# A streaming encoder layer on one core: when the operand sums of the output projection begin, and how two input projections are cut

## The chip, the cores and the metric

The kernel runs on one core of one Trainium2 chip. The time is the device time of one execution in microseconds (us); lower is better. A core has a matrix engine (TensorE, "PE" in the profile, with its weight loads as "PEld"), a vector engine (VectorE, "DVE"), a scalar engine (ScalarE, "ACT"), GpSimd ("POOL") and a queue that issues transfers (SyncE, "SP").

## The reference

One layer of a hybrid encoder, for 2048 prompt rows and 64 rows of a running stream, with model width 1024:

```python
aq, ak, av, ag, hq, hf, hi, hg = jnp.split(rms_norm(x, ln_g) @ w_in, SPLITS, axis=-1)
k, v = heads(ak), heads(av)
o_a = attn_fn(heads(aq), k, v).reshape(B, T, W_A) * jax.nn.silu(ag)
o_b, S = hgrn2_branch(hq, hf, hi, hg, lb, norm_g, s0)
y = x + jnp.concatenate([o_a, o_b], axis=-1) @ w_out
...
y_prompt, y_sample = rms_norm(hp, ln_f_g), rms_norm(hs, ln_f_g)
```

The input projection is 1024 by 4096 (eight groups of 512 columns). `attn_fn` is banded attention, 8 heads of 64, each 64-row chunk seeing itself and eight chunks before. `hgrn2_branch` is a gated linear recurrence with 4 heads of 128, whose gate is made of `hf` and whose query of `hq`. The output projection is 1024 by 1024, followed by the residual and a final RMS norm. New keys, values and recurrent states are outputs too. All arrays are float32; the kernel gets that accuracy by splitting each operand into a high part and a low remainder and adding three products.

## The kernel before

**Super-blocks and jobs.** The 2112 rows are worked in four super-blocks: 512, 576 (512 prompt rows and the 64 stream rows), 512 and 512. Each has 32 jobs, one for each 128 columns of the input projection. Job 0 is `hf` of head 0 (the forget gate), job 1 is `hq` of head 0 (the query). `project` (line 539) makes one job: 24 matmuls of 128 by 128 by the rows of a piece, 8 with the high weights and the high part `xh` of the normalized rows, 8 with the low part `xl`, 8 with the low weights and `xh`. The result goes to one of two accumulators `acc`, and a thread then moves it out of there: `ev_f` (line 1268) for `hf`, `silu_to` (line 566) for `hq`. Most jobs of the super-blocks of 512 rows are one piece of 512.

**The seam between two super-blocks.** `xh` and `xl` have one buffer. The rows of the next super-block are transposed into it in tiles of 128 rows (`x_tile`, line 351, and `x_split`, line 404: ACT writes `xh` on line 409, DVE writes `xl` on line 415) as soon as the last two jobs of this one have read their half (`x_left`). So the last two jobs of a super-block and the first two of the next are cut into halves of 256 rows (256 and 320 in the second super-block) and interleaved: job 0 half 0, job 1 half 0, job 0 half 1, job 1 half 1 (line 2092, with `u == 1`). `x_ready` (line 425) holds each of these pieces until the rows it reads are there.

**The output projection.** It is made for eight pairs of 128-row tiles (`pairs`, number i), each as a product of 2 by 2 blocks with seven block products instead of eight (`NPROD`, number k). For each pair four blocks a11, a12, a21, a22 are loaded; products 0, 1 and 6 read the blocks a11, a12 and a22 as loaded, and four sums are made in the same buffers:

- a11 = a11 - a21 on POOL, two instructions of 128 by 256
- a21 = a21 + a22 on DVE, one instruction of 128 by 512
- s2 = a22 - a11 on POOL, two instructions
- a12 = a12 - s2 on POOL, two instructions

Product 2 reads s2, product 3 the new a21, products 4 and 5 the new a11 and a12. For each product, `out_parts` (line 1729) has ACT copy the block to its high part (line 1751), and `out_low` (line 1755) subtracts it for the low part (line 1759): on POOL in two halves for pairs 0 and 1 except product 3, on DVE for the others. The sums stand at the end of `out_low`, under `k == 1`: the thread of product 1 makes them, on lines 1772 (DVE) and 1777 (POOL), and then marks them done in `sums_at`, for which the copy for product 2 waits. `out_step` (line 1821) makes 12 matmuls of 512 columns for each product, in the order of `steps` (line 1640): the products of pairs 0 and 1 interleaved, then pair by pair. `out_adds` (line 1859) adds a product to the residual rows (line 1847) or to a shared sum (lines 1865, 1873, 1852), and `out_norm` (line 1892) does the final norm (lines 1901 to 1926) and the store.

**Who sets the order.** The engines' instruction orders are written out when the program is made. A planner (`Plan`, line 52) keeps a clock of its own; every piece of work is a generator thread that yields what it waits for: a time, a token of a buffer, a condition, or a pair such as ("D", t), which means "time t, and DVE's queue no longer than 800 ns" (`QUEUE`). `pump` goes on with every thread whose wait is over, in the order of priority and then of age. The main thread, which issues the projections and the output products, lets the others in after every two matmuls. The planner's costs (`act`, `dve`, `pool`, `mm`) set the order alone; what the chip waits for are the data. So a thread that goes on earlier in the planner's clock puts its instructions further ahead in the queues of its engines, and everything after may fall in another order.

## Time and profile before

| | us |
|---|---|
| median of 3 runs | 1245.14 |
| lowest and highest | 1242.21, 1245.45 |
| the profiled execution | 1244.75 |
| its span, first to last instruction | 1243.0 |

| engine | busy us | share of the span | instructions |
|---|---|---|---|
| PE | 1229.9 | 99% | 7398 |
| PEld | 1079.5 | 87% | 7398 |
| DVE | 896.0 | 72% | 1897 |
| ACT | 680.2 | 55% | 1526 |
| POOL | 415.7 | 33% | 702 |

In rows of the timeline and the groups, "L1759" is line 1759, the name left of the arrow is the tile written, those right of it are read, and numbers in brackets at the end are idle time of the engine before the row and what ended it. A matmul's row gives its whole passage through the array, of which the next one overlaps a part; what a matmul costs in a stream is the distance from one start to the next. The projections of the third super-block start at about 539 us, those of the fourth at about 800 us; the output products run from 1056 us on, at first between the last attention blocks, from 1097 us on alone, and the last ends at 1236 us.

### The profile page before, as it was taken

To read this page: it belongs to the slowest core of one execution; us is meant where nothing else is said; L and a number is where in the kernel's file an instruction comes from. 1 tells how busy PE (TensorE), PEld (TensorE's weight loads), DVE (VectorE), ACT (ScalarE), POOL (GpSimd) and SP (SyncE) were. 2 spreads that over 40 slices of the span, in tenths; PEclk is the share of its full clock that TensorE was granted. 3 is DMA by queue.
4 is the path that set the end of the run, shared out by engine and by line. 5 is a ranking of instruction groups with operands and counts; after the bars stand their busy time and mean duration, and the time that the engine had idled before them with its cause. 6 is when DMAs were issued, how large, how long until landed. Compare 5 with 4: busy or idle time off the path is not lost.

```text
span 1243.0 us, 21228 instructions
## 1 busy us (share of the span) xinstructions
PE 1229.9 (99%) x7398; PEld 1079.5 (87%) x7398; DVE 896.0 (72%) x1897; ACT 680.2 (55%) x1526; POOL 415.7 (33%) x702
## 2 busy tenths in 40 slices
PE   9999999999999999999999999999999999999997
PEld 7888888999999999998888888988888888778786
DVE  7687878867767677786577667785768566866775
ACT  6354546755565556674455656664646444643443
POOL 7665564111120111201243242143242203664543
PEclk9999999999999999999999999999999999999999
DMA  8897988667575476655777878778878676987441
GB/s 338 302 321 258 322 292 330 204 183 253 155 219 147 153 248 197 197 165 188 274 270 252 283 264 266 238 245 270 272 274 249 222 244 211 352 257 225 128 136 67
DMA packets 158324, 294.36 MB, mean 237 GB/s; under 512 B 51657, under 2 KB 98377, under 8 KB 140554
## 3 DMA queue, kind: packets, MB, share of 16 engines
q1 hardware_dynamic: 157784, 292.74, 70.4%
q8 instruction: 58, 0.95, 0.3%
q14 instruction: 48, 0.39, 0.1%
q10 hardware_dynamic: 434, 0.27, 0.1%
HBM read 198.52 MB, written 95.49 MB: 237 GB/s over the span
## 4 chain that ended last, share of the span: by engine, by line
PE 92%; DMA 4%; DVE 3%; ACT 1%; issue 0%; SPq 0%; DVEq 0%; ACTq 0%
PE acc L249 61%; PE g L249 9%; PE pv L249 7%; PE tr L253 6%; PE s L249 5%; PE tr L249 3%; DMA out_dram<-ck 1%; DMA way<-vT 1%; DMA vT<-way 1%; PE g L253 1%; DMA w<-wd 0%; DMA mixd<-mixa 0%; DMA lbg<-in_lb_gamma_dram 0%; DMA bias<-wind 0%; ACT ck L1901 0%
## 5 line engine op out<-in xcount | busy, mean ns | idle before, releaser
L249 PE MATMUL acc<-xh,w 128*128 128x512 f32 (+2 forms) x2720 | 564.2, 347 | 0.8 <-ACT xh L409 0.7
L249 PEld LDWEIGHTS acc<-xh,w 128*128 128x128 f32 x2720 | 435.4, 189 | 51.6 <-ACT xh L409 0.9
L249 PE MATMUL acc<-xl,w 128*128 128x512 f32 (+2 forms) x1360 | 291.4, 346 | 0.5 <-DVE xl L415 0.5
L249 PEld LDWEIGHTS acc<-xl,w 128*128 128x128 f32 x1360 | 220.5, 189 | 26.5 <-DVE xl L415 0.7
L948 DVE CUSTOM_DVE_ANT_0 pr<-s,bias 128x640 f32<-128x640 f32 (+4 forms) x128 | 94.2, 736 | 53.1 <-PE s L249 52.6
L977 ACT CAST ph<-tr 128x512 fp32r<-128x512 f32 (+3 forms) x176 | 88.0, 506 | 75.6 <-PE pv L249 45.2
L965 ACT ACTIVATE pr<-pr,nm 128x640 f32<-128x640 f32 (+4 forms) x132 | 100.3, 760 | 52.4 <-DVE nm L948 52.0
L473 POOL TENSOR_TENSOR w<-wraw,w 128x256 fp32r<-128x256 f32 x120 | 102.3, 882 | 55.1 <-DVE w L468 41.8
L980 DVE TENSOR_TENSOR ph<-tr,ph 128x512 fp32r<-128x512 f32 (+3 forms) x176 | 100.8, 588 | 21.5 <-ACT ph L977 20.9
L249 PE MATMUL pv<-ph,v 128*128 128x256 f32 (+2 forms) x344 | 97.7, 370 | 0.9 <-DVE sm L968 0.7
L253 PE MATMUL tr<-ident,pr 128*128 128x128 f32 x580 | 88.3, 273 | 0.0
L1596 POOL TENSOR_TENSOR k<-ob 128x512 f32<-128x512 f32 (+2 forms) x20 | 18.0, 902 | 201.2 <-ACT ob L1587 163.2
L1121 POOL TENSOR_TENSOR mixa<-mixa,sga 128x256 f32<-128x256 f32 (+1 forms) x36 | 28.5, 792 | 167.9 <-DVE mixa L1019 142.2
L510 POOL TENSOR_TENSOR xn<-wraw,xn 128x256 fp32r<-128x256 f32 x48 | 40.2, 838 | 132.9 <-ACT xn L507 132.9
L969 DVE TENSOR_SCALAR pr<-pr,sm 128x640 f32<-128x640 f32 (+4 forms) x132 | 76.6, 580 | 4.7
L1019 DVE TENSOR_TENSOR mixa<-mixa,pv 64x256 f32<-64x256 f32 (+1 forms) x144 | 56.8, 394 | 30.7 <-ACT mixa L1015 27.1
L253 PEld LDWEIGHTS tr<-ident,pr 128*128 128x128 f32 x580 | 69.6, 140 | 10.3 <-DVE ph L980 1.1
L575 ACT ACTIVATE sig<-acc 128x512 f32<-128x512 f32 (+2 forms) x63 | 31.8, 505 | 73.4 <-PE acc L249 72.6
L249 PEld LDWEIGHTS pv<-ph,v 128*128 128x128 f32 (+1 forms) x344 | 58.3, 189 | 9.4 <-ACT pr L965 1.1
L1015 ACT COPY mixa<-pv 64x256 f32<-64x256 f32 (+1 forms) x72 | 25.1, 349 | 60.6 <-PE pv L249 54.7
L249 PE MATMUL s<-kd,q 128*128 128x320 f32 (+2 forms) x232 | 55.8, 311 | 0.2 <-DVE nm L948 0.2
L249 PE MATMUL s<-kd,ql 128*128 128x320 f32 (+2 forms) x232 | 55.5, 309 | 0.0
(414 smaller groups left out, 2126.0 us busy)
## 6 DMA issues: line engine op xcount, KB each, us to landing
w<-wd SPq DMA_DIRECT2D x96, 1024.0 KB, 5.8
wd<-w SPq DMA_DIRECT2D x32, 1024.0 KB, 7.1
wraw<-in_w_in_dram SPq DMA_DIRECT2D x30, 512.0 KB, 4.7
wod<-xn SPq DMA_DIRECT2D x28, 512.0 KB, 5.0
xn<-in_x_prompt_dram SPq DMA_DIRECT2D x23, 512.0 KB, 5.1
bias<-biasd SPq DMA_DIRECT2D x24, 320.0 KB, 5.7
carry<-kd SPq DMA_DIRECT2D x12, 512.0 KB, 6.2
carry<-v SPq DMA_DIRECT2D x12, 512.0 KB, 6.3
```

The lines of the kernel that those rows point to most:

```text
L249: pe.matmul(out, w, x, **kw)
L253: pe.transpose(out, x, idn)
L473: pool.tensor_sub(w[:, 1, k : k + 2], raw[:, k : k + 2], f32(w[:, 0, k : k + 2]))
L510: pool.tensor_sub(f32r(st[:, c.start + 512 : c.stop + 512]), src[:, c], st[:, c])
L575: act.activation(sig[:, :bn], acc, AF.Exp, scale=-1.0)
L948: dve.tensor_tensor_reduce(s[:, :nk].rearrange("p (a c) -> p a c", a=ns), sps[:, :ns, :kn], d.bias[:, h, bcol : bcol + nk].rearrange("p (a ...
L965: act.activation(s[:, :nk], s[:, :nk], AF.Exp, bias=nm[:, 0:1], scale=-1.0, accum_out=sm)
L969: dve.tensor_scalar(s[:, :nk], s[:, :nk], sm, None, ALU.mult)
L977: act.copy(ph[:krows, 0, :wid], pt[:krows, :wid])
L980: dve.tensor_sub(ph[:krows, 1, :wid], pt[:krows, :wid], f32(ph[:krows, 0, :wid]))
L1019: dve.tensor_add(mix[hs, :qn], mix[hs, :qn], pv[hs, i, :qn])
L1121: pool.tensor_mul(mix[:, :n], mix[:, :n], d.sg[:, g0 : g0 + n])
```

## The change

In the output projection the four sums move from the thread of product 1 to that of product 0, and only the last of them (into a12, which product 1 reads) still waits for product 1's low part. In the third and fourth super-block (`sb > 1`) job 0 is made alone in its two halves, and job 1 after it in one piece of 512; the first two super-blocks and the last two jobs of each stay as they were.

```diff
@@ out_low
         if k == NPROD - 1:
             for tag, n in tags.items():
                 tk[tag].put(n, t)
-        if k == 1:
+        if k == 0:
             (a11, a12, a21, a22), s2 = rows_at[i][:2]
-            yield lambda: (i, 0) in a_at
             for out, x, y, op in ((a11, a11, a21, ALU.subtract), (a21, a21, a22, ALU.add),
                                   (s2, a22, a11, ALU.subtract), (a12, a12, s2, ALU.subtract)):
                 if op == ALU.add:
...
                     dve.tensor_tensor(out, x, y, op)
                     C.dve(560, t)
                     continue
+                if out is a12:
+                    yield lambda: (i, 1) in a_at
                 for c in (slice(0, 2), slice(2, 4)):
                     yield "P", 0.0
                     pool.tensor_tensor(out[:, c], x[:, c], y[:, c], op)
@@ program
-                if u == 1 or (u == len(JOBS[sb]) - 1 and not last):
+                if sb > 1 and u == 0:
+                    for half in range(2):
+                        yield from project(j, [halves[half]], evac, half == 1,
+                                           lambda part, k0: x_ready(sb, half, part, k0))
+                elif u == 1 and sb < 2 or u == len(JOBS[sb]) - 1 and not last:
                     for half in range(2):
                         yield from project(j - 1, [halves[half]], before, half == 1,
                                            lambda part, k0: x_ready(sb, half, part, k0))
```

## The prediction, on record before the change was run

> **What bounds the kernel now.** I read the engines' busy times first, then what the matrix engine (PE) waited for, then stretches of time, then the order of time around the two places that the change touches.

> ```profile
> span 1243.0 us, 21228 instructions
> PE 1229.9 (99%) x7398; PEld 1079.5 (87%) x7398; DVE 896.0 (72%) x1897; ACT 680.2 (55%) x1526; POOL 415.7 (33%) x702
> ...
> PE 92%; DMA 4%; DVE 3%; ACT 1%; issue 0%; SPq 0%; DVEq 0%; ACTq 0%
> ```

> PE is busy in all but 13 us, and 92% of the chain that ended last is PE. So time can be won only by fewer or cheaper matmuls, or out of PE's few waits:

> ```profile
> PE acc L249 <- DVE slot L1759: 1.8, 1, 1.8
> ...
> PE pv L249 <- DVE sm L968: 0.7, 1, 0.7
> PE acc L249 <- ACT xh L409: 0.7, 2, 0.5
> PE acc L249 <- DMA w<-wod: 0.6, 1, 0.6
> ```

> The columns are total us, times, longest. The largest belongs to an output product that waited for a low part on DVE (L1759). The next two tables are of stretches: length, then busy time of PE, PEld, DVE, ACT and POOL, the granted clock, and the transfers.

> ```profile
> 538.00:558.00 20.00, 20.00 (x160) 19.61 (x159) 16.96 (x46) 15.63 (x39) 1.05 (x5) 1.00 0.50 161
> 800.00:820.00 20.00, 20.00 (x155) 19.33 (x155) 17.60 (x41) 16.76 (x42) 2.49 (x3) 1.00 0.76 243
> ...
> 830.00:1070.00 240.00, 238.40 (x1322) 201.48 (x1322) 159.98 (x317) 127.24 (x257) 67.95 (x106) 1.00 0.78 255
> ...
> 1116.20:1119.60 3.40, 1.61 (x7) 1.14 (x7) 3.40 (x6) 1.77 (x4) 0.00 (x0) 1.00 0.75 214
> 1119.60:1123.00 3.40, 3.40 (x10) 2.62 (x9) 2.42 (x6) 1.34 (x3) 0.06 (x1) 0.51 0.89 320
> 1123.00:1126.40 3.40, 3.40 (x16) 2.78 (x16) 1.48 (x3) 0.62 (x1) 3.40 (x5) 0.99 0.84 253
> ```

> At the two seams that the change cuts anew PE has no idle time at all. At 1116 us it idles, and right after that the granted clock is 0.51 for 3.4 us: 10 matmul records against 16 in the stretch behind it. The waits of 0.7 and 0.6 us (on L968 and on the transfer `w`) lie between 830 and 1070 us, where the clock stays at 1.00. So this one wait costs 1.8 us and about 3.4 x 0.49 = 1.7 us more, 3.5 us together.

> **Part 1, job 1 in one piece.** It takes 24 pairs of 256-column matmuls away in each of two super-blocks and puts 48 matmuls of 512 columns in their place. The price of each is read from the chain of waits, where these rows are unbroken streams: the first consists of 512-column matmuls alone, the second of 256-column ones.

> ```profile
> 563.87 8.64 PE acc L249 x38
> ...
> 807.43 3.35 PE acc L249 x28
> ```

> 8.64 / 38 = 227 ns, and 3.35 / 28 = 120 ns; two halves cost 239 ns against 227. 48 x 12 ns = 0.57 us are saved, all on the path, since PE is never idle there. [...]

> What it adds is a stricter order. Job 0's second half now follows its first half at once, where job 1's first half stood between them: 24 x 0.120 = 2.9 us less for the rows of the second half to arrive. In the fourth super-block they arrive so (PE's job 0 first, then the last writes of `xh` and `xl`):

> ```profile
> 800.40 1.11 PE L249 MATMUL acc<-xh,w 128*128 128x256 f32 x8
> 801.36 1.12 PE L249 MATMUL acc<-xl,w 128*128 128x256 f32 x8
> ...
> 803.83 1.43 PE L249 MATMUL acc<-xh,w 128*128 128x256 f32 x10
> ...
> 804.11 0.59 ACT L409 CAST xh<-g 128x512 fp32r<-128x512 f32 x1
> ...
> 804.44 0.69 DVE L415 TENSOR_TENSOR xl<-tr,xh 128x512 fp32r<-128x512 f32 x1
> 805.05 0.68 DVE L415 TENSOR_TENSOR xl<-g,xh 128x512 fp32r<-128x512 f32 x1
> ```

> Job 0's first half ends with the second matmul of the row at 803.83, at 804.07. Its second half would need the last piece of `xh` four matmuls later, at 804.55 (there at 804.70), the first of `xl` at 805.18 (there at 805.13), the last of `xl` at 805.66 (there at 805.73): 0.2 us of waits if nothing else stood between. In the third super-block the same margins are as close; I bound both seams together at 0 below, because score and transpose matmuls of the last attention pair stand between today and can go on doing so, and at 0.57 above, the whole of this part's gain. I take 0, being nearest to the stretches in which PE idles 0.00 us of 20. If that cover were gone, the loss is the 0.2 us per seam just worked out.

> Around it: `hq` is moved out of `acc` as one piece and not two, so the recurrence of head 0 begins a little later; the instructions saved are on ACT and DVE, which are not the bound. The accumulator turns over one time less, and job 0's weight buffer comes free a half-job (2.9 us) earlier, so the next weights are issued on SP no later than now. I put no cost or gain on these: PE's other work, 20.00 us in 20, hides them; without that cover the late `hq` would cost one extra half-piece on ACT and DVE, below 1 us.

> **Part 2, the sums.** No instruction is added or removed: six POOL pieces and one DVE sum per pair. They are put further ahead in the queues, by at most the time between the low parts of products 0 and 1. Where can that reach PE? Only where a low part came late, and there is one such place, product 2 of pair 2, which reads s2:

> ```profile
> 1109.09 0.68 DVE L1759 TENSOR_TENSOR xl<-wraw,xh 128x512 fp32r<-128x512 f32 x1
> ...
> 1109.91 1.77 POOL L1777 TENSOR_TENSOR wraw<-wraw,wraw 128x256 f32<-128x256 f32 x2 [5.84 <-DVE xl L1759]
> 1111.64 1.88 POOL L1777 TENSOR_TENSOR sga<-wraw,wraw 128x256 f32<-128x256 f32 x2
> ...
> 1114.81 0.57 ACT L1865 COPY asb<-pv 128x512 f32<-128x512 f32 x1
> 1115.27 0.62 ACT L1751 CAST slot<-sga 128x512 fp32r<-128x512 f32 x1
> ...
> 1115.22 1.76 DVE L1926 SCALAR_TENSOR_TENSOR bias<-bias,rstd,gin 128x1024 f32<-128x1024 f32 x1
> 1116.91 0.68 DVE L1847 TENSOR_TENSOR pr<-pr,pv 128x512 f32<-128x512 f32 x1
> 1117.51 0.68 DVE L1759 TENSOR_TENSOR slot<-sga,slot 128x512 fp32r<-128x512 f32 x1
> ...
> 1115.97 0.48 PE L249 MATMUL acc<-w,slot 128*128 128x512 f32 x1
> 1118.24 3.89 PE L249 MATMUL acc<-w,slot 128*128 128x512 f32 x11 [1.79 <-DVE slot L1759]
> ```

> Here `sga` is s2. POOL already starts the first sum 0.13 us after product 0's low part ends (1109.77), so as data s2 cannot come earlier: the move gains nothing on POOL. s2 is complete at 1113.52, but ACT copies it at 1115.27 and DVE subtracts it at 1117.51. In between stand the norm of pair 1 and the sums of pair 2 (L1865 on ACT; L1926, 1.76 us, and L1847, 0.60 us to the next start, on DVE). That is a matter of order. In the planner's costs one copy and one subtraction part the two low parts, but the copies were issued together here, so the sums come about half a microsecond earlier in the planner's clock. That is of the size that lets s2's low part pass one neighbour. The bounds: 0 if it passes none, -3.5 us if it passes both DVE neighbours (it then starts near 1115.9, when the copy is done, the wait falls below the 0.7 us waits that left the clock whole, and the half clock goes with it). I take one neighbour, L1847: -0.60 us, half clock kept. For pairs 3 to 7 PE shows no wait in the list above, so an earlier s2 is worth nothing.

> For pairs 0 and 1 the low parts are on POOL as well, and there the four pieces for a11 and s2 can now stand ahead of product 1's low part. For pair 1:

> ```profile
> 1071.63 1.20 POOL L1759 TENSOR_TENSOR slot<-sig,slot 128x256 fp32r<-128x256 f32 x1
> ...
> 1073.49 1.07 POOL L1759 TENSOR_TENSOR xl<-sig,xh 128x256 fp32r<-128x256 f32 x1
> ...
> 1075.21 1.69 POOL L1777 TENSOR_TENSOR sig<-sig,vT 128x256 f32<-128x256 f32 x2
> 1076.85 1.88 POOL L1777 TENSOR_TENSOR vT<-vT,sig 128x256 f32<-128x256 f32 x2
> ...
> 1077.99 0.39 PE L249 MATMUL acc<-w,xh 128*128 128x512 f32 x1
> ```

> The low part ends at 1074.56; PE's second matmul of that product, due one pitch after 1077.99, at 1078.22, reads it. The slack is 3.66 us, and the four pieces take 1.69 + 1.88 = 3.57 us. So it just fits: I take 0, with 1.2 us above (four pieces as slow as the one at 1071.63, 1.20 us, are 4.8 us). What is queued behind on POOL, the residual additions of L1852, has no PE reader.

> **The sum.** From the profiled execution: 1244.75 - 0.57 (pieces) + 0 (seams) - 0.60 (product 2 of pair 2) + 0 (pair 1) = 1243.58 us; I say 1243.6. The median of the runs shown, 1245.14, lies 0.39 above that execution, inside the 3.2 us between lowest and highest run. The likeliest case's own range is 1242.5 to 1244.8.

> **The rivals.**

> - **The wait at 1116 us goes altogether, and the half clock with it**: 1244.75 - 0.57 - 1.79 - 1.7 = 1240.7 us. For it: only two DVE instructions stand in the way, and part 1 shifts the planner's clock too, so that neighbours may change places in any case. Against it: the move is small, and s2 itself comes no earlier. [...]
> - **Nothing remains**: the seams eat the 0.57 us and s2's low part passes no neighbour: 1244.8 us. For it: margins of under 0.2 us at the seam. Against it: other PE work to fill them.
> - **Slower, by the POOL queue of pair 1**: product 1's low part stands behind the four sum pieces, and they take over 3.66 us together. At 4.8 us PE waits 1.2 us; as at 1116 us, a wait of this size can bring the half clock, 1.7 us more: 1244.75 - 0.57 + 1.2 + 1.7 = 1247.1 us. For it: the slack and the price agree within 0.1 us. Against it: attention matmuls stand between the products at that time and fill a wait.
> - **The sums do not start earlier at all** where PE needs them: for pair 2 the trace already shows that on POOL. It gives the first term alone, 1244.2 us, within the forecast's own range, and is counted there.

> **How the numbers follow.** Forecast 0.42, wait gone 0.28, nothing 0.15, slower by POOL 0.10; 0.05 for a new wait anywhere else, by the new order, at the end. 0.3% (3.7 us), about what a measurement of this kernel can tell from no change, puts the bounds at 1241.4 and 1248.9. Below lies the case of the wait gone, and a little of the forecast when other short waits (0.7 and 0.6 us) fall out of the new order too: 0.30. Above lies only a POOL wait or a new one of twice the size worked out: 0.08. Within: 0.62. The range goes from 1239.9, the wait gone and one of the short waits with it, to 1247.2.

> **What would show it.** The groups by form now have

> ```profile
> L249 PE MATMUL acc<-xh,w 128*128 128x256 f32 x832 | 123.6, 286 | 0.2 <-ACT xh L409 0.2
> ...
> L249 PE MATMUL acc<-xl,w 128*128 128x256 f32 x416 | 63.1, 286 | 0.5 <-DVE xl L415 0.5
> ```

> Right: 64 and 32 of these 832 and 416 matmuls are gone, and 48 of 512 columns more are there; no PE wait on L409 or L415 at the third and fourth seam. For the sums: in the list of PE's waits the L1759 row falls below 1.8 us, or goes, and in DVE's order s2's subtraction stands ahead of L1847 or L1926. Wrong: PE idle at the seams; a PE wait on POOL L1759 near 1078 us; a second stretch with the clock near half; or an end that moves by more than 4 us without any of these, which would mean that the planner's new order did it and not these terms.

## The result, and the profile after

| | before | after |
|---|---|---|
| median of four runs each, us | 1244.3 | 1250.44 |
| lowest and highest | 1242.21, 1245.45 | 1249.28, 1250.65 |
| profiled execution, us | 1244.75 | 1250.3 |
| its span, us | 1243.0 | 1248.5 |

The ratio is 1.0051, with a 95% interval of 1.0038 to 1.0063: the change makes the kernel about 6 us slower. Predicted were 1243.6 us and a range of 1239.9 to 1247.2. The time lies outside the range, on the side that had a chance of 0.08.

The head of the profile page after, and the shares of the chain that ended last:

```profile
span 1248.5 us, 21107 instructions
...
PE 1230.2 (99%) x7350; PEld 1076.2 (86%) x7350; DVE 898.1 (72%) x1895; ACT 680.1 (54%) x1520; POOL 408.3 (33%) x702
...
PE 93%; DMA 3%; DVE 2%; ACT 1%; issue 0%; SPq 0%; POOL 0%; DVEq 0%; ACTq 0%; POOLq 0%
```

PE has 48 matmuls fewer (7350 against 7398), as the change intends, and is busy for as long as before; the span is 5.5 us longer. To see where, I cut both executions into the same stretches. The columns are length, then busy time of PE, PEld, DVE, ACT and POOL, granted clock, and transfers; the last stretch ends with the last matmul. Before:

```profile
10.00:520.00 510.00, 508.65 (x3428) 466.57 (x3426) 384.23 (x900) 284.86 (x666) 173.09 (x336) 1.00 0.71 240
520.00:830.00 310.00, 309.98 (x1897) 272.50 (x1896) 224.66 (x476) 186.08 (x404) 74.86 (x134) 1.00 0.72 244
830.00:1010.00 180.00, 179.83 (x983) 152.55 (x983) 120.11 (x234) 95.79 (x193) 53.76 (x90) 1.00 0.80 259
1010.00:1090.00 80.00, 78.45 (x445) 64.86 (x444) 57.05 (x120) 44.86 (x95) 31.05 (x36) 1.00 0.80 276
1090.00:1236.40 146.40, 144.57 (x629) 117.43 (x627) 103.39 (x157) 60.91 (x153) 76.84 (x90) 0.99 0.51 159
```

After:

```profile
10.00:520.00 510.00, 508.16 (x3422) 465.85 (x3421) 384.63 (x898) 284.98 (x666) 173.06 (x335) 1.00 0.72 240
520.00:830.00 310.00, 310.00 (x1852) 269.65 (x1851) 226.53 (x474) 184.71 (x398) 71.56 (x131) 1.00 0.73 243
830.00:1010.00 180.00, 178.85 (x979) 151.51 (x978) 120.82 (x236) 94.00 (x190) 51.40 (x94) 1.00 0.80 255
1010.00:1090.00 80.00, 73.03 (x408) 60.01 (x407) 51.25 (x111) 41.81 (x87) 23.36 (x27) 0.98 0.73 255
1090.00:1241.90 151.90, 151.63 (x673) 123.62 (x671) 108.20 (x167) 66.95 (x164) 82.66 (x100) 1.00 0.53 172
```

Both seams lie in 520 to 830 us, where PE is never idle. Between 1010 and 1090 us, the end of the fourth super-block, PE lost 5.42 us (78.45 - 73.03) and the clock fell to 0.98. Behind that, PE's idle time went from 1.83 to 0.27 us: the wait at 1116 us is nearly gone. The change in idle time is thus +0.49 (10 to 520), -0.02, +0.98, +5.42 and -1.56, together +5.3 us. With 0.57 us for the pieces that makes 4.7 of the 5.5 us by which the last matmul ends later (1241.9 against 1236.4); the rest was not placed. Each execution has one stretch ahead of the last matmul in which the granted clock is 0.50, and both are 3.41 us long (1119.64 to 1123.06 us before, 1075.27 to 1078.68 us after), so the half clock is as long in both, in another place (PE is busy for 3.41 and 2.86 us of it). The 0.49 us are mostly one gap of 0.74 us near 123 us, where the two programs do not differ yet.

PE's waits of the kernel after (total us, times, longest) name what ended these gaps:

```profile
PE tr L253 <- DVE pr L969: 3.2, 1, 3.2
PE pv L249 <- DVE ph L980: 1.7, 1, 1.7
...
PE g L249 <- ACT k L1522: 1.1, 1, 1.1
...
PE acc L249 <- DVE slot L1759: 0.3, 1, 0.3
```

PE waited for the softmax on DVE, and DVE in turn for ACT. So the view to read is ACT's own waits for transfers between 1010 and 1085 us. Before, beside two of 2.4 and 0.3 us (on L1901 and L1751):

```profile
ACT gi L1305 <- DMA vT<-way: 5.0, 1, 5.0
```

After:

```profile
ACT sig L575 <- DMA out_dram<-sig: 5.6, 1, 5.6
ACT gi L1305 <- DMA vT<-way: 4.3, 1, 4.3
```

**The first wait, at L575.** Line 575 is the first instruction of the gate of the last attention pair (`silu_to`). It works in one of two `sig` buffers. After the change that buffer still holds new K rows whose store is under way. The timeline of ACT, DVE and PE there (start, length, instruction, idle time before it):

```profile
1065.47 1.08 ACT L977 CAST ph<-tr 128x512 fp32r<-128x512 f32 x2 [0.89 <-PE tr L253]
1072.16 0.60 ACT L575 ACTIVATE sig<-acc 128x512 f32<-128x512 f32 x1 [5.61 <-DMA out_dram<-sig]
...
1074.08 0.81 ACT L965 ACTIVATE pr<-pr,nm 128x640 f32<-128x640 f32 x1
...
1075.21 0.55 DVE L969 TENSOR_SCALAR pr<-pr,sm 128x640 f32<-128x640 f32 x1
...
1075.82 0.90 PE L253 MATMUL tr<-ident,pr 128*128 128x128 f32 x3 [3.19 <-DVE pr L969]
```

ACT stands for 5.61 us. Behind the gate on the same engine stands a softmax exponential (L965) that needs nothing of that buffer; it runs at 1074.08, DVE normalizes it at 1075.21 and PE transposes it at 1075.82. The store itself, as the chain that ended last has it:

```profile
1062.47 9.58 DMA out_dram<-sig
```

It landed 9.58 us after its issue. The planner hands the buffer on 6 us after the issue (line 655, `C.now + (6000.0 if rows == P else 0.0)`), so in its clock the gate finds the buffer free. Who gets which buffer is settled in the planner's clock too:

```
the planner's clock, us                              before      after
gate of the last pair is issued, on a sig buffer     1036.100    1043.684
first load of output pair 1 (sig<-mixd) has its own  1039.431    1036.913
```

Before, the gate came first, and on the chip it waited for its matmuls alone. After, the loads pass it, and the gate is left with the buffer of the stores.

**The second wait, at L1305.** Line 1305 copies the `hi` rows of a recurrence head after they have come back from DRAM. ACT waits for them in both kernels; what stands behind differs. Before:

```profile
1019.53 0.62 ACT L1305 COPY gi<-vT 128x512 f32<-128x512 f32 x1 [4.99 <-DMA vT<-way]
1020.06 0.83 ACT L965 ACTIVATE pr<-pr,nm 128x640 f32<-128x640 f32 x1
...
1022.24 0.47 PE L249 MATMUL pv<-ph,v 128*128 128x256 f32 x2 [0.72 <-DVE sm L968]
```

After:

```profile
1023.75 0.62 ACT L1305 COPY gi<-vT 128x512 f32<-128x512 f32 x1 [4.32 <-DMA vT<-way]
1024.39 1.07 ACT L977 CAST ph<-tr 128x512 fp32r<-128x512 f32 x2
...
1025.76 0.73 PE L249 MATMUL pv<-ph,v 128*128 128x512 f32 x2 [1.66 <-DVE ph L980]
```

The wait is even shorter, but PE loses 1.66 us and not 0.72; what has come to stand behind it are two casts (`ph`, L977), whose low part DVE makes on L980 and which PE's next product needs at once.

### The profile page after: what moved, and what is told of

Same layout as the page of the kernel before. It is cut to its first block, busy times and chain, and to the rows that moved or that the text cites. A ratio compares the mean times of both kernels' runs of the same rounds, so it can differ in the third digit from the quotient of the medians.

```text
span 1248.5 us, 21107 instructions
## 1 busy us (share of the span) xinstructions
PE 1230.2 (99%) x7350; PEld 1076.2 (86%) x7350; DVE 898.1 (72%) x1895; ACT 680.1 (54%) x1520; POOL 408.3 (33%) x702
## 4 chain that ended last, share of the span: by engine, by line
PE 93%; DMA 3%; DVE 2%; ACT 1%; issue 0%; SPq 0%; POOL 0%; DVEq 0%; ACTq 0%; POOLq 0%
PE acc L249 61%; PE g L249 9%; PE pv L249 7%; PE tr L253 6%; PE s L249 6%; PE tr L249 4%; DMA kd<-carry 1%; DMA out_dram<-sig 1%; DMA wod<-xn 1%; PE g L253 1%; DMA bl<-way 1%; DMA vT<-way 0%; DVE pr L948 0%; ACT xh L409 0%; ACT ck L368 0%
## 5 line engine op out<-in xcount | busy, mean ns | idle before, releaser
L249 PE MATMUL acc<-xh,w 128*128 128x512 f32 (+2 forms) x2688 | 568.3, 349 | 0.6 <-ACT xh L409 0.5
L249 PEld LDWEIGHTS acc<-xh,w 128*128 128x128 f32 x2688 | 431.7, 189 | 51.9 <-ACT xh L409 0.9
L249 PE MATMUL acc<-xl,w 128*128 128x512 f32 (+2 forms) x1344 | 290.9, 348 | 0.5 <-DVE xl L415 0.5
L249 PEld LDWEIGHTS acc<-xl,w 128*128 128x128 f32 x1344 | 219.0, 189 | 26.4 <-DVE xl L415 0.7
L965 ACT ACTIVATE pr<-pr,nm 128x640 f32<-128x640 f32 (+4 forms) x132 | 100.4, 760 | 80.8 <-DVE nm L948 80.3
L980 DVE TENSOR_TENSOR ph<-tr,ph 128x512 fp32r<-128x512 f32 (+3 forms) x176 | 100.9, 587 | 24.9 <-ACT ph L977 24.2
L977 ACT CAST ph<-tr 128x512 fp32r<-128x512 f32 (+3 forms) x176 | 87.4, 505 | 53.4 <-PE pv L249 31.9
L249 PE MATMUL pv<-ph,v 128*128 128x256 f32 (+2 forms) x344 | 96.8, 368 | 2.2 <-DVE ph L980 1.7
L969 DVE TENSOR_SCALAR pr<-pr,sm 128x640 f32<-128x640 f32 (+4 forms) x132 | 79.2, 600 | 4.7
L575 ACT ACTIVATE sig<-acc 128x512 f32<-128x512 f32 (+2 forms) x61 | 31.6, 518 | 77.3 <-PE acc L249 71.1
L249 PEld LDWEIGHTS pv<-ph,v 128*128 128x128 f32 (+1 forms) x344 | 58.9, 189 | 11.1 <-DVE ph L980 2.3
L249 PE MATMUL s<-kd,q 128*128 128x320 f32 (+2 forms) x232 | 56.4, 313 | 1.4 <-DVE nm L948 1.3
L249 PE MATMUL s<-kd,ql 128*128 128x320 f32 (+2 forms) x232 | 55.5, 309 | 0.0
```

What stands on the lines that cost most here:

```text
L249: pe.matmul(out, w, x, **kw)
L575: act.activation(sig[:, :bn], acc, AF.Exp, scale=-1.0)
L965: act.activation(s[:, :nk], s[:, :nk], AF.Exp, bias=nm[:, 0:1], scale=-1.0, accum_out=sm)
L969: dve.tensor_scalar(s[:, :nk], s[:, :nk], sm, None, ALU.mult)
L977: act.copy(ph[:krows, 0, :wid], pt[:krows, :wid])
L980: dve.tensor_sub(ph[:krows, 1, :wid], pt[:krows, :wid], f32(ph[:krows, 0, :wid]))
```

## The experiments

They ran in four groups, each on one chip with the kernel before beside it, and every median is set beside that of the kernel before in the same group.

**1. Each part alone.** The theory at that point was that the gate's wait at L575 comes from a new order that the pieces bring; the rivals, that the sums or the pieces cost time themselves.

The pieces alone leave the sums with product 1:

```diff
-                if u == 1 or (u == len(JOBS[sb]) - 1 and not last):
+                if sb > 1 and u == 0:
+                    ...
+                elif u == 1 and sb < 2 or u == len(JOBS[sb]) - 1 and not last:
```

> Job 1 in one piece, the sums as before. Theory 'gate': with the changed kernel's planner order the silu of the last gate (pair 3) gets its sig buffer only after the loads of product pair 1, waits on ACT 5.6 us for the store of the new K rows (3.19 us of PE idle, and the half clock, 1.7 us), and this comes from the pieces; so this kernel is slower than before by 4 to 8 us, with an ACT wait of over 4 us at L575 for out_dram<-sig. Rival 'sums' (the earlier sums block DVE or POOL and delay the last attention blocks): about 0.6 us faster than before.

The sums alone leave job 1 in halves:

```diff
-        if k == 1:
+        if k == 0:
...
+                if out is a12:
+                    yield lambda: (i, 1) in a_at
```

> The sums begin behind product 0, job 1 in halves as before. Theory 'gate': the gate's silu stands where it stood, no wait at L575; the time is between 3.5 us faster and equal to before, by what becomes of the wait at product 2 of pair 2. Rival 'sums': slower by 4 to 6 us, as the whole change.

Measured: the pieces alone 1252.09 us against 1244.1, ratio 1.0060 (1.0044 to 1.0076); the sums alone 1244.42, ratio 1.0001 (0.9992 to 1.0011). So the loss comes with the pieces. ACT's waits for transfers between 1010 and 1085 us with the pieces alone:

```profile
ACT sig L575 <- DMA out_dram<-sig: 6.0, 1, 6.0
ACT gi L1305 <- DMA vT<-way: 4.7, 1, 4.7
```

and PE's waits:

```profile
PE tr L253 <- DVE pr L969: 3.2, 1, 3.2
...
PE acc L249 <- DVE slot L1759: 1.3, 1, 1.3
```

The first two are the waits of the whole change, and PE stands as long behind the gate. With the sums alone ACT has no wait at L575 (and 4.4 us at L1305), and PE's wait for s2's low part is what it was before:

```profile
PE acc L249 <- DVE slot L1759: 1.8, 1, 1.8
```

**2. The gate's wait taken away, the rest of the order kept.** The gate of the last pair works in its own output room and takes no `sig` buffer; the planner still counts one, so that all engines have the instructions of the kernel after in the same order.

```diff
+            if own_room:
+                sig = dst()[:, off:]
+            else:
                 sig = T(wk, [P, 512], F32, "sig", bufs=2)
...
-        gate = silu_to(sg, sga_free)
+        gate = silu_to(sg, sga_free, last and p == NPAIR - 1)
```

> The whole change, with every instruction in the same order on every engine; only the last gate's silu (L575 to L577, pair 3) writes its three steps into its own result buffer sga instead of a sig buffer, so that it doesn't wait for the store of the K rows. Theory 'gate': 4 to 5 us faster than the changed kernel (3.19 + 1.7), so within 0 to 2 us of before, with no PE wait on L969 near 1073 us. Rivals 'sums' and 'many small waits': as the changed kernel, about 6 us slower than before.

Measured: 1247.51 us, ratio 1.0030 (1.0013 to 1.0047). The row of L575 is gone from ACT's waits, and 0.2 to 0.4% with it (1.0051 - 1.0030, or 1.0066 - 1.0030 with the second measurement of the change in experiment 5). The ten runs lie between 1244.02 and 1253.31 us, and the intervals overlap, so this difference alone would not prove the gain. A loss of 0.3% stays, where at most 2 us was expected. Of the two waits the second is left (its line is 1308 in this kernel). ACT's wait, and in the timeline PE's product behind it:

```profile
ACT gi L1308 <- DMA vT<-way: 5.3, 1, 5.3
```

```profile
1024.99 0.73 PE L249 MATMUL pv<-ph,v 128*128 128x512 f32 x2 [2.65 <-DVE ph L983]
```

So the theory of one cause fell here: the gate is only a part of it.

**3. The loads of pair 1 behind the gate.** The whole change, and the loads wait until the gate has its buffer, which is the order of before at this place.

```diff
+            if last and p == NPAIR - 1:
+                have.add("gated")
...
-            yield lambda: "projected" in have
+            yield lambda: "projected" in have and "gated" in have
```

> The whole change, and the loads of product pair 1 wait until the last gate's silu is issued (one more condition for the planner, no instruction added); the gate gets the free sig buffer, as before the change. Theory 'gate': no wait at L575, 4 to 6 us faster than the changed kernel, so between 1.5 us faster and 1.5 us slower than before. Rivals: as the changed kernel.

Measured: 1247.79 us, ratio 1.0031 (1.0019 to 1.0044). The wait at L575 is gone in this way too, with the same gain; the expectation, within 1.5 us of before, was missed. The wait at the copy of `hi` (L1307 here) is still there, 4.6 us, and the order moves again: PE now has a gap of 2.1 us near 1080 us, behind a `ph` piece of DVE, and one of 1.9 us for s2's low part. This run confirms the place of the wait; it says little on the rest.

**4. The planner's clock moved, the work as before.** The kernel before, with its 24 pairs of half pieces; only the planner's clock is set 290 ns back, or on, after job 1 of the third and fourth super-block. 290 ns is what the prediction had one piece save (24 x 12 ns).

```diff
+                        if u == 1 and sb > 1 and half:
+                            C.now -= 290.0
```

> The kernel before with the same matmuls, in halves as they were; only the planner's own clock is set back by 290 ns after the second job of super-blocks three and four, as if the merged piece's saving had been booked. Theory 'order' (the pieces cost nothing as work; the shift of the planner's clock brings another order at the end of the fourth super-block, with ACT waiting for two transfers): slower than before by 3 to 8 us, with ACT waits at L575 for the store of K rows and at L1305, and PE waits near 1023 and 1074 us. Rival 'work' (the merged piece itself delays its evacuation and the recurrence): as before, within 1 us.

and with `C.now += 290.0`:

> The same with the planner's clock set forward by 290 ns. Theory 'order', and that the order of the kernel before is one of a few good ones: slower than before by 3 to 8 us with the same two ACT waits, though the shift has the other sign. Rival 'a saving of the planner's clock brings it': as before or faster.

Measured: 1252.97 us (1.0063, 1.0043 to 1.0083) and 1254.76 us (1.0085, 1.0064 to 1.0105) against 1245.23. ACT's waits with the clock set back:

```profile
ACT sig L575 <- DMA out_dram<-sig: 5.1, 1, 5.1
ACT gi L1305 <- DMA vT<-way: 4.6, 1, 4.6
```

With the clock set on they are 5.4 and 4.3 us. No matmul was changed, both signs bring the same two waits, and the loss is that of the change or, with the clock set on, more. So the 512 columns as such need not cost anything: a shift of the planner's clock by as much, with the work left alone, costs as much or more. The order of before is a favourable one, with worse ones at 290 ns on both sides. In the planner's clock of both shifted kernels the loads and the gate ask for a `sig` buffer at the same moment (1035.870 us set back, 1037.030 us set on), as in the change (1036.913 us), and the loads are served first; before, the gate asked at 1034.982 us and the loads at 1037.475 us. What brings the two together was not followed further back.

**5. Both waits taken away, on the change and on before.** The edit of experiment 2, and L1305 of head 3 in the last super-block on POOL:

```diff
-                    act.copy(r.iv[...], it[...])
+                    (pool.tensor_copy if sb == nsb - 1 and h == NHB - 1 else act.copy)(r.iv[...], it[...])
```

> The whole change with both ACT waits taken away, in the planner's order of the changed kernel: the last gate's silu works in its own result buffer, and the copy of hi's rows into gi (L1305) of head 3 in the fourth super-block is made by POOL and not by ACT, so that ACT does not stand in line behind that transfer. Theory 'order': 5 to 8 us faster than the changed kernel, so between 1.5 us faster and 1 us slower than before; no PE wait of over 1 us near 1023 or 1074 us. Rival 'one wait goes, another takes its place': about 3 us slower than before, as with the gate alone.

> The kernel before with the same two edits. Its ACT waits 5.0 us at L1305 as well, but PE lost only 0.72 us there, and its gate doesn't wait. Theory 'order': 0 to 1.5 us faster than before. Rival: slower, if POOL's copy delays the sums or the gi rows are needed earlier.

The second edit alone, on the change, and the whole change once more:

> The whole change with the copy L1305 of head 3 (fourth super-block) on POOL alone; the last gate's silu still takes a sig buffer. Theory 'two ACT waits add up': with the gate alone taken away the loss fell from about 6 to 3.5 us, with both to -2 us; so this one should be 2 to 3.5 us slower than before, with the wait at L575 (5 us or more) and PE's 3.2 us on L969 still there and no PE wait near 1023 us. Rival 'only the two together help': 5 us slower or more.

> The whole change once more, on the same chip as the two halves of it. All theories: about 6 us slower than before, with the ACT wait of over 5 us at L575 and a PE wait of about 3.2 us on L969 behind it.

Measured, as ratios to before:

| the whole change | L575 waits | L575 does not |
|---|---|---|
| L1305 on ACT | 1.0051 (1.0038 to 1.0063), again 1.0066 (1.0046 to 1.0085) | 1.0030 (1.0013 to 1.0047) |
| L1305 on POOL | 1.0031 (1.0021 to 1.0041) | 0.9984 (0.9975 to 0.9993) |

The cells come from different groups, each against its own kernel before. Each edit takes off between 0.2 and 0.5%, alone or beside the other, so within the intervals the two add up. With L1305 alone on POOL (1248.40 us against 1243.98, a little slower than expected) ACT's wait of 5.4 us at L575 and PE's of 3.2 us on L969 are still there, and PE has no gap near 1023 us. With both gone the change is faster than before, 1243.33 us against 1245.23. The same two edits on the kernel before bring nothing: 1244.61, ratio 0.9999 (0.9988 to 1.0009). PE and SP have the same instructions in the same order in all four cells, and so has DVE but for the buffer that the gate's product reads. So the edits mend what the new order brought. The profile of the change with both edits has no wait of ACT for a transfer between 1010 and 1085 us. Its span is 1241.5 us. On POOL, as the timeline has it, the copy waits where nothing stands close behind it (between 1015 and 1027 us it is POOL's only instruction):

```profile
1022.63 0.61 POOL L1308 COPY gi<-vT 128x512 f32<-128x512 f32 x1 [29.78 <-DMA vT<-way]
```

**6. The piece in one super-block alone.** Both with the sums moved:

```diff
+                if sb == 2 and u == 0:
+                    ...
+                elif u == 1 and sb != 2 or u == len(JOBS[sb]) - 1 and not last:
```

> The earlier sums, and job 1 in one piece in the third super-block alone. In the planner's order the last gate's silu gets its sig buffer ahead of the loads of product pair 1, as in the kernel before. Theory 'order': no ACT wait at L575 for the store, so within 2.5 us of before (the wait behind L1305 can still cost up to 2 us of PE and a half clock). Rival 'the pieces as such': slower by about half of the whole change's loss, 3 us, with the L575 wait or not.

and with 3 in place of 2:

> The earlier sums, and job 1 in one piece in the fourth super-block alone. In the planner's order the gate is ahead too, and the last jobs (123 to 127) stand as they did before the change. Theory 'order': no ACT wait at L575, within 1.5 us of before. Rival 'the pieces as such': about 3 us slower.

Measured: in the third alone 1242.93 us, ratio 0.9995 (0.9982 to 1.0009); in the fourth alone 1249.07, ratio 1.0042 (1.0029 to 1.0054). The second was a miss: I had expected it within 1.5 us of before, since its gate does not wait at L575. It waits longer at L1305 instead, and PE with it. ACT's waits and PE's:

```profile
ACT gi L1305 <- DMA vT<-way: 6.7, 1, 6.7
```

```profile
PE pv L249 <- DVE sm L968: 2.5, 1, 2.5
```

**7. L1305 on POOL with these two.** The edit of experiment 5 at L1305 on the fourth alone, and both edits on the third alone:

> The earlier sums and the piece in the fourth super-block alone (5.2 us slower than before, with no wait at L575), and L1305 of head 3 on POOL. Theory 'ACT behind the transfer of hi': 4 to 6 us faster than without the last edit, so within 1.5 us of before. Rival 'something else in that order': faster by 2.5 us at most (the PE wait of 2.46 us near 1021), so 2.5 us slower than before or more.

> The earlier sums, the piece in the third super-block alone, and both ACT waits taken away. Without those two edits it was 0.6 us (0.05%) faster than before, with an ACT wait of 5.8 us at L1305 and a PE wait of 2.0 us near 1025. Theory 'ACT behind the transfer of hi': 1 to 4 us faster than before. Rival: as before.

Measured: 1243.92 us, ratio 0.9997 (0.9987 to 1.0007), and 1242.98, ratio 0.9992 (0.9981 to 1.0003). In the fourth super-block the whole loss of the piece went with that one wait. The third alone stays where it was without the edits, and neither can be told from before: the 1 to 4 us that I expected to gain did not show. The profile of the third alone does have a wait of 5.8 us at L1305, a gap of 2.0 us on PE behind it and a half clock after that, but that execution took 1247.54 us against a median of 1242.93. Whether its usual executions have the gap is not known.

## Why the prediction was wrong, point by point

**The piece of 512 columns: the count was right, its gain stays below what these runs resolve.** The groups by form after:

```profile
L249 PE MATMUL acc<-xh,w 128*128 128x256 f32 x768 | 114.3, 287 | 0.1
...
L249 PE MATMUL acc<-xl,w 128*128 128x256 f32 x384 | 58.4, 286 | 0.5 <-DVE xl L415 0.5
```

64 and 32 of these matmuls are gone, as counted. The term of -0.57 us is smaller than every interval above (0.1% is 1.2 us).

**The seams: right at 0.** PE is busy for 310.00 of 310 us from 520 to 830, with no wait on L409 or L415 there.

**The POOL queue of pair 1, the case forecast as slower: it did not come.** PE's waits have no row on POOL L1759. The price given to that case also held a half clock behind a wait of 1.2 us, an estimate from the 1.79 us at 1116 us that the change did not bear out: after it, the gaps of 1.15 us near 914 us and 1.66 us near 1024 us were followed by a clock of 1.00 (see the last section).

**Product 2 of pair 2: the term of -0.60 us was wrong in its cause and its size.** The prediction had the earlier sums carry s2's low part past one neighbour on DVE. The sums alone left the wait at 1.8 us. With both parts it fell from 1.79 to 0.25 us, and no half clock followed (1.00 from 1078.68 to 1242 us), but the low part passed neither neighbour:

```profile
1122.85 0.69 DVE L1848 TENSOR_TENSOR pr<-pr,pv 128x512 f32<-128x512 f32 x1 [0.43 <-ACT asb L1866]
1123.45 1.28 DVE L1927 SCALAR_TENSOR_TENSOR bias<-bias,rstd,gin 128x1024 f32<-128x1024 f32 x1
1124.65 0.69 DVE L1759 TENSOR_TENSOR slot<-sga,slot 128x512 fp32r<-128x512 f32 x1
```

These are the prediction's L1847 and L1926 (one line further down here), in the other order, and the norm took 1.28 us and not 1.76. What shifted is the place of the whole chain against PE: ACT's copy of s2 starts 0.68 us after the first of PE's twelve matmuls of the product ahead (1122.71 against 1122.03), where before it started 2.02 us after (1115.27 against 1113.25). What the first rival promised did happen at this place (all but 0.25 us of the wait gone, and its half clock of 1.7 us), but neither part did it alone (1.8 us with the sums, 1.3 us with the pieces), and which turn in the order did it was not traced. The measured loss is what is left after this gain.

**The failed step is "I put no cost or gain on these: PE's other work ... hides them".** It was argued from two stretches of 20 us in the middle of the seams, and holds there. But every instruction whose turn moves in the planner's clock moves all that comes after, up to the end of the fourth super-block, and there the cover ends: the last projections run out, attention and output products alternate, and ACT stands in front of transfers. The prediction read PE's waits and the seams. It did not read ACT's waits for transfers, though the kernel before had one of 5.0 us on L1305 that cost PE only 0.72 us, by what happened to stand behind it. The case of "a new wait anywhere else, by the new order" had 0.05. By these runs it was the likely one. Five orders that differ from that of before ahead of the two waits were run without the edits: the piece in both super-blocks, in the third, in the fourth, the clock set back and set on. Four of them were slower by 0.4% or more. The sums alone do not count here: ACT's order in that kernel is that of before up to 1077 us, behind both places.

The prediction's own test for this held: the end moved by more than 4 us, with no idle PE at the seams, no wait on POOL, and no second stretch near half clock (the one there is has moved). It named that outcome as the planner's new order, and gave it too little.

## What to carry to other kernels

Where an order of instructions is written out by a planner, a small change can move any later instruction, so read not only the waits of the bound engine but also every long wait for a transfer on the engines that feed it, and what stands behind each; a wait can become costly as soon as the order may change: the one at L1305, 5.0 us before, cost PE 0.72 us there, and after the change, at 4.3 us, it cost 1.66. Before a planned order is credited or blamed, shift the planner's clock by the size of the change with the work left alone: here plus and minus 290 ns gave the whole loss or more. An instruction that waits for a transfer belongs on an engine with nothing urgent behind it (L1305 on POOL took the fourth super-block's piece from 1.0042 to 0.9997), and a buffer that a slow store holds (9.58 us here) should not be shared with work on the path.

## What the runs showed of the hardware

**Where the half clock fell.** Beside its stretch at 0.50 ahead of the last matmul (3.41 us), each of the executions before and after has one behind it, from 1239.11 and from 1245.94 us. The two starts lie 119.47 us apart before and 170.67 us after, 35 and 50 times 3.413 us. So I cut both executions into stretches of 3.413 us, counted from those starts, and set PE's busy time in each beside the clock in the next. Before, the stretch with most idle time between matmuls had 1.79 us (1.62 us busy), and the next ran at 0.50; the second had 0.72 us, and the next ran at 1.00. After, 2.63 us (0.78 us busy) was followed by 0.50, and 1.66 us (1.75 us busy, the gap near 1024 us) by 1.00. Other executions, cut to the same length; first the sums alone:

```profile
1113.72:1117.13 3.41, 3.12 (x13) 2.06 (x11) 3.41 (x3) 3.07 (x8) 2.58 (x3) 1.00 1.01 376
1117.13:1120.55 3.42, 1.91 (x8) 1.61 (x9) 3.42 (x7) 1.36 (x4) 0.00 (x0) 1.00 0.74 204
1120.55:1123.96 3.41, 3.41 (x16) 2.81 (x16) 2.32 (x5) 1.21 (x3) 1.01 (x2) 1.00 0.92 311
```

The piece in the fourth super-block alone, with a gap of the same length:

```profile
1117.61:1121.03 3.42, 1.62 (x7) 0.86 (x6) 3.42 (x5) 2.70 (x6) 0.64 (x1) 1.00 0.66 207
1121.03:1124.44 3.41, 3.41 (x10) 2.66 (x9) 2.51 (x5) 0.72 (x2) 0.00 (x0) 0.50 0.96 291
...
1018.63:1022.04 3.41, 2.29 (x12) 1.52 (x11) 0.00 (x0) 1.37 (x4) 0.00 (x0) 1.00 0.57 219
1022.04:1025.46 3.42, 2.08 (x12) 1.83 (x13) 2.28 (x6) 3.33 (x8) 0.00 (x0) 1.00 0.72 122
1025.46:1028.87 3.41, 3.41 (x20) 2.98 (x20) 3.08 (x9) 1.31 (x3) 0.00 (x0) 1.00 0.66 267
```

Both kernels have a gap of 1.80 us, near 1117 us in the first and near 1119 us in the second. In the first, 0.29 us of it fall into the stretch ahead (3.12 of 3.41 us busy), PE is busy for 1.91 us of the next, and the clock stays at 1.00. In the second all of it falls into one stretch, PE is busy for 1.62 us, and the next runs at 0.50. The gap of 2.46 us near 1021 us of the second kernel is cut by a boundary (2.29 and 2.08 us busy), and the clock stays at 1.00.

**The store at the end of the fourth super-block takes 9.6 us** from issue to landing. In the kernel before it took 9.6 us too, with no instruction of ACT waiting for it; in four of the runs whose gate waits for it, 9.6 (the whole change), 10.7 (once more), 10.0 (the pieces alone) and 9.1 us (the clock set back). The issues of the kernel after between 1058 and 1073 us (size of each, median from issue to landing):

```profile
w<-wod SPq DMA_DIRECT2D x2, 1024.0 KB, 8.3
...
out_dram<-sig SPq DMA_DIRECT2D x1, 256.0 KB, 9.6
```

SP issues the store of 256 KB at 1062.47 us, right behind the two loads of weights (1061.53 us). Whether it waits for those was not tried.

What stays open: the gap of 1.15 us near 914 us (L1522) was 0.3 us when the whole change ran again, with the same order of instructions, and is not explained; nor is the last microsecond or so of the shift.
